# Six gate tiles of the second branch, made later as three pairs by seven quadrant products; piece sums moved to VectorE

## The chip, the cores and the metric

One core of a Trainium2 chip. The metric is device time in microseconds of one execution, as the median of repeated runs. The engines are TensorE (PE; its weight loads are PEld), VectorE (DVE), ScalarE (ACT), GpSimd (POOL) and SyncE (SP), whose queue issues almost all DMAs. All arithmetic is on float32 data; a matmul operand is split into a rounded high part and a low remainder (`wh`/`wl`, `xh`/`xl`, `th`/`tl` ...), and a product is three matmuls: high by high, high by low, low by high.

## The reference

One encoder layer over two sequences of 512 tokens with 1024 channels, with two memories of 256 tokens:

```python
xn = _rmsnorm(x, norm_mix);  h = xn @ w_in
u, q, k, v, xq, g = split(h)             # g: three gates of 1024 columns
y_s5 = s5(u)                             # state-space scan in two directions, gelu, glu
y_diff = diff_attention(q, k, v)         # 4 heads of two softmax maps, their difference
y_x = cross_attention(xq, memory)        # 4 heads
merged = sum(sigmoid(g[n]) * (branch[n] @ w_up[n]) for n in range(3))
x = x + merged @ w_out
gate, up = split(rmsnorm(x, norm_ffn) @ w_ffn_in)
x = x + (silu(gate) * up) @ w_ffn_out;   out = rmsnorm(x, norm_final)
```

## The kernel before, in words

Channels lie on the 128 partitions and tokens along the free axis: `xh[k]`, `xl[k]` (k from 0 to 7) are the normalised x, both sequences side by side in 1024 columns. An output tile of a projection (128 channels, both sequences) takes a weight tile of 512 KB (`weight`: DMA to `wf`, cast to `wh` on ScalarE, remainder `wl` on VectorE; two slots each) and 2 sequences by 8 k by 3 matmuls of 128x512.

The gates are 24 such tiles, drawn in order from the iterator `todo` (line 394); tile t is stored in HBM as `gD[t]`, and branch n uses tiles 8n to 8n+7. They serve as TensorE work beside what other engines do:

- `gates(n)` (400) makes n tiles at once. `NG = (7, 6, 3)` (42): 7 and 2 tiles ahead of the state-space scan, 4 between pieces of the scan, which VectorE does; then lines 420 to 424 put 0, 1 and 1 ahead of three steps of the scan's generator `s5` that make the scan's outputs (`behind()` lets a step's instructions follow the matmuls traced last). After them the outputs go to HBM (`yD`), are loaded again (`zu`, `zy`, lines 502 and 503), and pass through gelu into `zh`, `zl` (504 to 511); `gates(NG[2])`, three tiles, stands behind these lines and ahead of the projection by `w_glu`, which reads `zh`, `zl` by four contraction steps.
- Cross attention (690 to 726) runs 32 steps of scores, softmax, transpose and product, and between them `fill(n)` (590) takes n matmuls from `queue`, a list of generators. There the queue holds `xq` projections 1 to 3, two gate tiles, v for half the heads and the first q, 384 matmuls; a step takes 3 + 3 and what is left follows the last step.
- Differential attention has a second queue: q, k and v projections, three gate tiles and `merges()`. Ahead of its first scores (829) stand the first k projection and one gate tile. From line 679 to 921 TensorE keeps the written order (`PE.on`); elsewhere a planner with a cost model orders each engine's instructions.

`merges()` (794) holds the merge units of branches 0 and 2 (8 output tiles each, 24 matmuls a tile): load the gate (`gl`, from `gD`), multiply it with the product on VectorE (line 779), add into `mg[m]` on POOL (783). Those of branch 1 follow the queue, with 6 PSUM banks in place of 2. The operand of branch 1 is loaded and split in `merges()` (m = 2 to 5) and behind it. All loads of this kind, x parts and gate tiles share four slots of the tag `ld`.

Then come `w_out`, and the feed-forward input as 22 sweep steps. There a pair of tiles (one of gate, one of up, or two halves of channels by two sequences) is made by seven quadrant products in place of eight: operands 0 to 6 are four sums and differences of the quadrants of x beside three of them, weights A11, A12, A22 and S1 to S4 come from two weight tiles (`weights4`, 1003; the four sums of 128x512 on POOL, lines 1023 to 1026), and `running` (1120) accumulates four of the seven in one bank with copies between. A product is 4 k by 3 matmuls; a sweep step is 84.

Beside the sweep, `prepare` (457) makes the weights of 28 (m, p) pieces of the feed-forward output: load a piece (`raw`, four blocks of 128x128), four sums on POOL (`raw_sums`, 449, lines 452 to 455), split into `hl`, store to HBM (`wD`). The first 16 pieces store all seven weights, the next 12 the four sums alone. `half_piece` (489) does half a piece of the first kind or one of the second; it is called three times in a sweep step.

```python
    for n in (0, 1, 1):
        gates(n)
        with behind():
            next(s5)
```

Of the kernel before, what the change touches and what calls it, by code (L numbers as in the profile page):

```python
# [10 lines left out]
F32 = mybir.dt.float32  # L11
# [8 lines left out]
P = 128  # L20
# [20 lines left out]

NG = (7, 6, 3)

# [29 lines left out]
def encoder(ctx: ExitStack, tc: tile.TileContext, a, out):  # L73
# [319 lines left out]

    todo = iter(range(24))

# [52 lines left out]

    def raw_sums(raw):

        a21, a11, a12, a22 = (raw[:, i] for i in range(4))
        PO.tensor_tensor(out=a22, in0=a21, in1=a22, op=ALU.add)
        PO.tensor_tensor(out=a21, in0=a11, in1=a21, op=ALU.subtract)
        PO.tensor_tensor(out=a11, in0=a22, in1=a11, op=ALU.subtract)
        return PO.tensor_tensor(out=a12, in0=a12, in1=a11, op=ALU.subtract)

    def prepare(es_, todo_):
# [144 lines left out]
    def finish(g):  # L602
        while any(g is g_ for g_ in queue):
            fill(1)
# [78 lines left out]
    for i in range(-AHEAD, len(steps) + 1):  # L683
        if i + AHEAD < len(steps):
# [11 lines left out]
            es[i + AHEAD] = e  # L696
        fill(9 if i == 0 else 3)
        if 0 <= i < len(steps):
# [71 lines left out]
    def merge_units(n, b, m, first=False, last=False):  # L770
# [13 lines left out]
        if last:  # L784
            mgh[m] = slot("ms", [P, NT], F32R, f"mgh{m}")
            mgl[m] = slot("ms", [P, NT], F32R, f"mgl{m}")
            split(mgh[m], mgl[m], mg[m])
# [3 lines left out]
    b2_in = []  # L791
    b1_in = []

    def merges():
        res_.close()
        xp_es.close()
        open_tags(mes, side="right", mg=8, y=8)
        for m in range(KD):
            yield from merge_units(0, b0, m, first=True)
            if 3 <= m < 7:  # L800
                with tc.issue_after(last_s[0].ins):
                    merge_split(b2, 2, m - 3, "y", b2_in[m - 3])
            if 2 <= m < 6:
                b2_in.append(merge_load(2, m - 2))
        for m in range(KD):
            yield from merge_units(2, b2, m)
            if m == 2:
                open_tags(zes, side="right", z=4)
            if m in (2, 3):
                merge_split(b1, 1, m - 2, "z", merge_load(1, m - 2))  # L810
            elif m in (4, 5):
                b1_in.append(merge_load(1, m - 2))

# [10 lines left out]
    v1_ = v_units(1, v1)  # L824
    queue += [qk_units(1, True), dk[1], gate_units(), qk_units(2, True), dk[2], v1_, qk_units(3, True), dk[3], gate_units(),
              gate_units(), merges()]
    s0, ss, osb = {}, {}, {}

# [88 lines left out]
    aes.close()  # L917
    while queue:
        fill(24)
    assert next(todo, None) is None  # L920
    PE.on = False
    phase.close()
    ves.close()


    open_banks(mm=6, tr=2)
    open_tags(phase, ms=16)
    ves = ExitStack()
    open_tags(ves, y1=4)
    for t, yt in zip((2, 3), b1_in):  # L930
        merge_split(b1, 1, t, "y1", yt)
    for m in range(KD):
# [5 lines left out]


    zes.close()  # L940
    mes.close()
    ves.close()
    tes = ExitStack()
# [55 lines left out]

    H = 4 * P  # L1000
    last_ws = None

    def weights4(i):

        nonlocal last_w, last_ws
        a1, a2 = (wp.tile([P, DM], F32, tag="wf", name="wf") for _ in range(2))
        nc.sync.dma_start(a1, a["w_fg"][i])
        last_w = nc.sync.dma_start(a2, a["w_fu"][i])
        res = {}

        def sp(pool, src, sfx, *names):
            n = len(names) * H
            nonlocal last_s
            wh, wl = (pool.tile([P, DM], F32R, tag=t_ + sfx, name=t_, bufs=2) for t_ in ("wh", "wl"))
            last_s = split(wh[:, :n], wl[:, :n], src)
            for j, nm in enumerate(names):
                res[nm] = (wh[:, j * H : (j + 1) * H], wl[:, j * H : (j + 1) * H])

        sp(wp, a1, "", "A11", "A12")
        sp(wp, a2[:, H:], "", "A22")  # L1020
        yield res
        s12, s34 = (slot("ld", name="ws") for _ in range(2))
        PO.tensor_tensor(out=s12[:, :H], in0=a2[:, :H], in1=a2[:, H:], op=ALU.add)
        PO.tensor_tensor(out=s12[:, H:], in0=s12[:, :H], in1=a1[:, :H], op=ALU.subtract)  # L1024
        last_ws = PO.tensor_tensor(out=s34[:, H:], in0=a1[:, H:], in1=s12[:, H:], op=ALU.subtract)
        PO.tensor_tensor(out=s34[:, :H], in0=a1[:, :H], in1=a2[:, :H], op=ALU.subtract)
        yield
        sp(aps, s12, "s", "S1", "S2")
        sp(aps, s34, "s", "S3", "S4")
        yield  # L1030

# [30 lines left out]
    def product(ps, w, o, ks=range(4), on=False):  # L1062
        wh, wl = w
        for k in ks:
            th, tl = ops[k]
            ws_ = slice(k * P, (k + 1) * P)
            PE.matmul(ps, wh[:, ws_], th[:, o], start=(k == 0 and not on), stop=False, skip_group_check=on)
            PE.matmul(ps, wh[:, ws_], tl[:, o], start=False, stop=False, skip_group_check=on)
            PE.matmul(ps, wl[:, ws_], th[:, o], start=False, stop=(k == 3), skip_group_check=on)

    SEVEN = (("A11", 0), ("S2", 4), ("A12", 1), ("S3", 5), ("S1", 3), ("A22", 6), ("S4", 2))

    def products(i, w):
# [24 lines left out]
    last_sum = last_c = None  # L1098

# [791 lines left out]
```

## Time and profile before

| what | value |
|---|---|
| median of 3 runs | 1606.28 us (1604.17 to 1607.21) |
| profiled execution | 1605.93 us, its span 1604.1 us |
| mean granted TensorE clock | 0.998 |
| busy PE / PEld / DVE / ACT / POOL | 1578.0 / 1308.9 / 1116.0 / 648.0 / 495.2 us |
| HBM read, written | 165.16 MB, 71.27 MB |

The profile is of one execution. Busy time is the union of an engine's records; a matmul's record is longer than the spacing of matmuls, since they are pipelined, so that PE can read as busy without a gap at less than its best rate. In rows of groups stand the line, the engine, the operation, out<-in with shapes, the count, then busy us and mean ns of one, then the idle time of that engine before them and what ended it. In rows of waits stand who waited <- for whom, us in total, times, the longest. In rows in order of time stand start and duration in us.

### The profile page before, as it was taken

What the parts mean: (1) busy time and instruction counts of PE and PEld (TensorE: products, weight loads), DVE (VectorE), ACT (ScalarE), POOL (GpSimd) and SP (SyncE); (2) the same over time, 40 slices, a digit from 0 to 9 for tenths busy, and PEclk for the clock granted to TensorE, in tenths of its full rate; (3) what the DMA queues carried; (4) which work ended last, traced back from release to release, by engine and by line L of the source; (5) the groups of instructions that cost most, each with busy time, mean ns of one, the idle gap of its engine ahead of it and who ended that gap; (6) DMA issues with size and microseconds to landing.
All of it is one profiled execution on the core that took longest, in us unless ns stands there. A gap on an engine that the chain in (4) does not pass through costs nothing. (4 is left out here: it accounts for less than half of the span.)

```text
span 1604.1 us, 21458 instructions
## 1 busy us (share of the span) xinstructions
PE 1578.0 (98%) x7738; PEld 1308.9 (82%) x7738; DVE 1116.0 (70%) x1821; ACT 648.0 (40%) x1153; POOL 495.2 (31%) x415
## 2 busy tenths in 40 slices
PE   9999999999999999999999999999998999999998
PEld 7888888888898788778888888777776887888877
DVE  7978994086553876865555587777767666988864
ACT  6544213275442455754124354333333333233323
POOL 0010000000002320300452445555767334434673
PEclk9999999999999999999999999999999999999999
DMA  9554533573111211145534434445455323785412
GB/s 356 184 174 131 189 107 128 174 276 107 60 66 57 88 57 44 34 158 178 197 125 142 134 112 149 174 167 176 158 181 171 127 97 122 290 324 189 165 60 106
DMA packets 108842, 237.84 MB, mean 148 GB/s; under 512 B 14016, under 2 KB 45760, under 8 KB 108736
## 3 DMA queue, kind: packets, MB, share of 16 engines
q1 hardware_dynamic: 108160, 236.06, 43.4%
q8 instruction: 61, 1.00, 0.3%
q10 hardware_dynamic: 576, 0.41, 0.1%
q14 instruction: 45, 0.37, 0.1%
HBM read 165.16 MB, written 71.27 MB: 147 GB/s over the span
## 5 line engine op out<-in xcount | busy, mean ns | idle before, releaser
L66 PE MATMUL bkmm<-xh,wh 128*128 128x512 f32 x640 | 254.6, 398 | 0.0
L66 PE MATMUL bkmm<-xh,wl 128*128 128x512 f32 x640 | 250.4, 391 | 0.0
L66 PE MATMUL bkmm<-xl,wh 128*128 128x512 f32 x640 | 250.1, 391 | 0.0
L66 PE MATMUL bkmm<-th,wl 128*128 128x512 f32 (+1 forms) x621 | 237.3, 390 | 12.4 <-DVE wl L135 12.4
L66 PE MATMUL bkmm<-th,wh 128*128 128x512 f32 (+1 forms) x621 | 239.7, 390 | 1.8 <-ACT u L1128 1.0
L66 PE MATMUL bkmm<-tl,wh 128*128 128x512 f32 (+1 forms) x621 | 241.2, 388 | 0.0
L135 DVE TENSOR_TENSOR wl<-wf,wh 128x1024 fp32r<-128x1024 f32 (+2 forms) x134 | 153.0, 1141 | 77.5 <-ACT wh L134 73.0
L134 ACT CAST wh<-wf 128x1024 fp32r<-128x1024 f32 (+2 forms) x134 | 117.3, 875 | 171.1 <-PE bkmm L66 159.1
L744 POOL TENSOR_TENSOR t<-t,rs 128x512 f32<-128x512 f32 x16 | 26.6, 1665 | 461.1 <-DVE t L743 461.1
L66 PEld LDWEIGHTS bkmm<-th,wl 128*128 128x128 f32 x621 | 116.5, 188 | 40.7 <-DVE wl L135 17.0
L66 PE MATMUL bkmm<-th,w 128*128 128x512 f32 x432 | 141.0, 392 | 1.9 <-DVE nsq L1103 1.2
L66 PEld LDWEIGHTS bkmm<-xh,wh 128*128 128x128 f32 x640 | 120.3, 188 | 26.8 <-issue 3.5
L66 PEld LDWEIGHTS bkmm<-xh,wl 128*128 128x128 f32 x640 | 120.2, 188 | 26.0 <-issue 0.4
L66 PEld LDWEIGHTS bkmm<-xl,wh 128*128 128x128 f32 x640 | 120.4, 188 | 22.8
L66 PEld LDWEIGHTS bkmm<-th,wh 128*128 128x128 f32 x621 | 116.6, 188 | 27.2 <-ACT u L1128 2.1
L66 PEld LDWEIGHTS bkmm<-tl,wh 128*128 128x128 f32 x621 | 116.6, 188 | 24.0
L135 DVE TENSOR_TENSOR wl<-ws,wh 128x1024 fp32r<-128x1024 f32 x44 | 59.5, 1352 | 73.6 <-ACT wh L134 73.6
L66 PEld LDWEIGHTS bkmm<-th,w 128*128 128x128 f32 x432 | 80.9, 188 | 22.7 <-DVE nsq L1103 2.1
L134 ACT CAST wh<-ws 128x1024 fp32r<-128x1024 f32 x44 | 46.0, 1045 | 111.7 <-POOL ws L1024 105.4
L783 POOL TENSOR_TENSOR mg<-mg,gl 128x1024 f32<-128x1024 f32 x16 | 43.8, 2740 | 136.8 <-DVE gl L779 132.1
L66 PE MATMUL bkmm<-tl,w 128*128 128x512 f32 x216 | 84.1, 389 | 0.0
L66 PE MATMUL bkmm<-yh,wh 128*128 128x512 f32 x192 | 76.2, 397 | 0.0
(666 smaller groups left out, 3448.5 us busy)
## 6 DMA issues: line engine op xcount, KB each, us to landing
wf<-in_w_in SPq DMA_DIRECT2D x40, 512.0 KB, 3.7
wD<-hl SPq DMA_DIRECT2D x28, 512.0 KB, 3.2
w<-wD SPq DMA_DIRECT2D x28, 512.0 KB, 4.8
gD<-gt SPq DMA_DIRECT2D x24, 512.0 KB, 2.8
gl<-gD SPq DMA_DIRECT2D x24, 512.0 KB, 3.5
wf<-in_w_fg SPq DMA_DIRECT2D x22, 512.0 KB, 3.4
wf<-in_w_fu SPq DMA_DIRECT2D x22, 512.0 KB, 3.7
aD<-ac SPq DMA_DIRECT2D x44, 256.0 KB, 2.2
```

The costliest lines, as they stand in the source:

```text
L66: return self.put(self.eng.matmul(*args, **kw))
L134: h = S.copy(hi, src)
L135: l_ = V.tensor_tensor(out=lo, in0=src, in1=hi.bitcast(F32), op=ALU.subtract)
L744: PO.tensor_tensor(out=t2, in0=t2, in1=rope[1], op=ALU.mult)
L783: PO.tensor_tensor(out=mg[m], in0=mg[m], in1=gt, op=ALU.add)
```

## The change

Gate tiles 10 to 15 (branch 1, m = 2 to 7) leave `todo`. In their places: `NG` becomes (7, 6, 1), the loop ahead of the scan outputs (0, 0, 1), the queue of cross attention loses two gates and `fill` takes 4 + 4 a step, the gate ahead of the first differential scores goes. The normalised x of both sequences is stored in HBM (`xnD`, 4 MB) once it is made. When the merge units of branch 0 are done, the rest of the queue (branch 2) (`merges2`; `first_` is `merges0`, branch 0) runs alternately with `operands_x`, which loads x back and makes the seven operand pieces `xop` on VectorE and ScalarE. Behind the queue three pairs of tiles are made by `gate_pair`: 84 matmuls each, weights by `quad_weights` (the former `weights4`) with the four sums on VectorE, and `tanh` on ScalarE. The operand of branch 1 is then loaded and split, and its merge units follow. The output weights' piece sums in `prepare` run on VectorE in place of POOL; the feed-forward sweep itself keeps POOL for its weight sums.

```diff
-NG = (7, 6, 3)
+NG = (7, 6, 1)
+LATE = (2, 3, 4, 5, 6, 7)
...
+    xnD = drp.tile([NS, KD, P, L], F32, name="xnD")
...
         x_norm(0, norm[0], range(5, 8))
         _, bc = factor(ss1, DM)
+    nc.sync.dma_start(xnD[0].rearrange("k p n -> p k n"), xt[2])
...
         x_norm(1, bc, range(5, 8))
+    for i in range(4):
+        nc.sync.dma_start(xnD[1, 2 * i : 2 * i + 2].rearrange("k p n -> p k n"), xt[3][i])
...
-    todo = iter(range(24))
+    todo = iter([t for t in range(24) if t - KD not in LATE])
...
-    for n in (0, 1, 1):
+    for n in (0, 0, 1):
...
-    def raw_sums(raw):
+    def raw_sums(raw, eng=PO):
         a21, a11, a12, a22 = (raw[:, i] for i in range(4))
-        PO.tensor_tensor(out=a22, in0=a21, in1=a22, op=ALU.add)
+        eng.tensor_tensor(out=a22, in0=a21, in1=a22, op=ALU.add)
...
             if k == 7 or n_ == 0:
-                raw_sums(raws[n_])
+                raw_sums(raws[n_], V)
                 yield
             part(n_, 0, raws[n_])
             if n_ + 1 < len(todo_) and todo_[n_ + 1][2] == 4:
-                raw_sums(raws[n_ + 1])
+                raw_sums(raws[n_ + 1], V)
...
-    queue += [xq[1], gate_units(), xq[2], xq[3], v_units(0, v0), gate_units(), units(a["w_in"][4], xh, xl, dq0.__setitem__)]
+    queue += [xq[1], xq[2], xq[3], v_units(0, v0), units(a["w_in"][4], xh, xl, dq0.__setitem__)]
...
-        fill(9 if i == 0 else 3)
+        fill(9 if i == 0 else 4)
...
-        fill(3 if i < len(steps) else 15)
+        fill(4 if i < len(steps) else 15)
...
-    for _ in gate_units():
-        pass
...
+    finish(first_)
+    phase.close()
+    ves.close()
+    open_tags(phase, ta=8)
+    open_tags(qes, tb=4)
+    open_tags(ges, tt=1)
...
+    def operands_x():
+        rooms = [pieces_of("tb", 0, 2), pieces_of("ta", 3, 2), pieces_of("ta", 5, 2)]
+        for k in range(4):
+            x1_, x2_ = slot("ld", [P, 2, L], name="xa"), slot("ld", [P, 2, L], name="xb")
+            for s, t_ in enumerate((x1_, x2_)):
+                nc.sync.dma_start(t_, xnD[s, k::4].rearrange("a p n -> p a n"))
+            split(*next(rooms[0]), x1_)
+            t_ = slot("tt", [P, 4, L], name="tt")
+            V.tensor_tensor(out=t_[:, 0], in0=x2_[:, 0], in1=x1_[:, 0], op=ALU.subtract)
+            V.tensor_tensor(out=t_[:, 1], in0=x2_[:, 1], in1=t_[:, 0], op=ALU.subtract)
+            yield
+            V.tensor_tensor(out=t_[:, 2], in0=x2_[:, 1], in1=x2_[:, 0], op=ALU.subtract)
+            V.tensor_tensor(out=t_[:, 3], in0=x1_[:, 1], in1=t_[:, 1], op=ALU.subtract)
+            split(*next(rooms[1]), t_[:, 0:2])
+            split(*next(rooms[2]), t_[:, 2:4])
+            yield
+    parts = operands_x()
     while queue:
+        next(parts, None)
         fill(24)
+    for _ in parts:
+        pass
...
+    def gate_pair(m):
+        w = None
+        for r_ in quad_weights(a["w_in"][20 + KD + m], a["w_in"][20 + KD + m + 1], sps, V):
+            w = w or r_
+        g1, g2 = slot("ld", name="gp"), slot("ld", name="gp")
...
+        run = bank()
+        prod(run, "A11", 0)
+        u1 = kept_sum("u1")
+        p_ = bank()
+        prod(p_, "A12", 1)
+        gated(g1[:, :L], p_, u1)
+        prod(run, "S2", 4, True)
+        u2 = kept_sum("u2")
+        p5 = bank()
+        prod(p5, "S1", 3)
+        u4 = gps.tile([P, L], F32, tag="u1", name="u4")
+        V.tensor_tensor(out=u4, in0=p5, in1=u2, op=ALU.add)
+        prod(run, "S3", 5, True)
+        u3 = kept_sum("u3")
+        gated(g2[:, L:], p5, u3)
+        p_ = bank()
+        prod(p_, "S4", 2)
+        gated(g1[:, L:], p_, u4)
+        prod(run, "A22", 6, True)
+        S.activation(out=g2[:, :L], in_=run, func=AF.Tanh, scale=0.5)
+        for j, g_ in enumerate((g1, g2)):
+            nc.sync.dma_start(gD[KD + m + j], g_)
+
+    for m in LATE[::2]:
+        gate_pair(m)
+    for t in range(4):
+        hl = slot("tb", [P, 2, NT], F32R, f"1{t}")
+        b1[0][t], b1[1][t] = hl[:, 0], hl[:, 1]
+        split(*(b_[t] for b_ in b1), merge_load(1, t))
     for m in range(KD):
         for _ in merge_units(1, b1, m, last=True):
             pass
```

More of the change, by code (lines that the diff above doesn't have):

```diff
@@ L784, in merge_units @@
         if last:
[L785 to L786 removed]
+            hl = slot("ta", [P, 2, NT], F32R, f"mg{m}")
+            mgh[m], mgl[m] = hl[:, 0], hl[:, 1]
             split(mgh[m], mgl[m], mg[m])
@@ new lines, in encoder @@
+    gps = ges.enter_context(tc.tile_pool(name="gps", bufs=1, reuse_waits="tile"))
+    open_banks(mm=6, tr=2)
+    late = [slot("tc", [P, 4, L], F32R, n_) for n_ in ("lh", "ll")]
+    for k in range(0, 4, 2):
+        x_ = slot("ld", [P, 2, L], name="xc")
+        nc.sync.dma_start(x_, xnD[1, k + 4 : k + 6].rearrange("a p n -> p a n"))
+        split(*(t_[:, k : k + 2] for t_ in late), x_)
+        for j in range(2):
+            xop[2, k + j] = tuple(t_[:, k + j] for t_ in late)
+    H = 4 * P
@@ new lines, in quad_product, with prod, kept_sum, gated @@
+    def quad_product(op, ps, w, o, ks=range(4), on=False):
+        wh, wl = w
+        for k in ks:
+            th, tl = op(k, o)
+            ws_ = slice(k * P, (k + 1) * P)
+            PE.matmul(ps, wh[:, ws_], th, start=(k == 0 and not on), stop=False, skip_group_check=on)
+            PE.matmul(ps, wh[:, ws_], tl, start=False, stop=False, skip_group_check=on)
+            PE.matmul(ps, wl[:, ws_], th, start=False, stop=(k == 3), skip_group_check=on)
+    def gate_pair(m):
[3 more added lines that the diff above has]
+        g1, g2 = slot("ld", name="gp"), slot("ld", name="gp")
+        def prod(ps, nm, o, on=False):
+            quad_product(lambda k, o_: xop[o_, k], ps, w[nm], o, on=on)
+        def kept_sum(tag):
+            t_ = gps.tile([P, L], F32, tag=tag, name=tag)
+            S.copy(t_, run)
+            return t_
+        def gated(dst, p_, other):
+            V.tensor_tensor(out=dst, in0=p_, in1=other, op=ALU.add)
+            S.activation(out=dst, in_=dst, func=AF.Tanh, scale=0.5)
+        run = bank()
[20 more added lines that the diff above has]
+            nc.sync.dma_start(gD[KD + m + j], g_)
@@ L998, in operands @@
         return quad_split(i, xa_, xb_, quad_sums(xa_, xb_, third=third))
-    H = 4 * P
-    last_ws = None
     def weights4(i):
[L1005 to L1030, printed above, removed]
+        return quad_weights(a["w_fg"][i], a["w_fu"][i], aps, PO)
     ops = []
@@ L1062, in product @@
     def product(ps, w, o, ks=range(4), on=False):
[L1063 to L1069, printed above, removed]
+        quad_product(lambda k, o_: tuple(t_[:, o_] for t_ in ops[k]), ps, w, o, ks, on)
     SEVEN = (("A11", 0), ("S2", 4), ("A12", 1), ("S3", 5), ("S1", 3), ("A22", 6), ("S4", 2))
```

72 lines of the change are left out of this document (50 added, 22 removed).

## The prediction

> **What bounds the kernel now.** I read the page first, then the busy time by stretches, then the order of instructions where the edit lands.
>
> ```profile
> span 1604.1 us, 21458 instructions
> PE 1578.0 (98%) x7738; PEld 1308.9 (82%) x7738; DVE 1116.0 (70%) x1821; ACT 648.0 (40%) x1153; POOL 495.2 (31%) x415
> ...
> 312.50:345.20 32.70, 32.70 (x146) 27.08 (x146) 21.91 (x36) 16.71 (x23) 0.00 (x0) 1.00 0.74 262
> ...
> 757.00:801.00 44.00, 44.00 (x196) 36.13 (x196) 22.80 (x31) 9.86 (x19) 19.06 (x7) 1.00 0.59 192
> 991.00:1149.00 158.00, 153.62 (x673) 125.61 (x672) 118.38 (x144) 61.41 (x96) 93.72 (x93) 1.00 0.50 170
> 1149.00:1237.00 88.00, 79.17 (x340) 62.91 (x339) 63.11 (x72) 32.63 (x49) 68.26 (x72) 1.00 0.51 171
> 1256.00:1332.00 76.00, 76.00 (x337) 62.94 (x336) 49.32 (x65) 27.38 (x39) 28.24 (x20) 1.00 0.29 97
> ...
> 1560.00:1604.00 44.00, 36.92 (x272) 34.93 (x270) 19.43 (x42) 14.40 (x34) 17.42 (x21) 0.94 0.26 96
> ```
>
> The columns are the stretch, its length, then busy time with instruction count of PE, PEld, DVE, ACT, POOL, the granted clock, DMA share, GB/s. TensorE sets the end nearly everywhere. Its price of one 128x512 matmul is not the busy time of a record but the spacing: 76.00 us for 337 in 1256:1332, so 0.2255 us. At that price the two stretches before it should hold 700.6 and 390.2 matmuls and hold 673 and 340: 27.6 and 50.2 missing, 6.2 and 11.3 us, together 17.5 us of TensorE standing still. Those are the sweep steps of the feed-forward input in which the output weights are prepared as well.
>
> **The count of products.** Before, each of the six tiles is 2 sequences by 8 steps by 3 matmuls, 48; six are 288. After, each of three pairs is 7 products by 4 steps by 3, 84; three are 252. Minus 36 matmuls is 36 x 0.2255 = -8.1 us, if the late pairs run at TensorE's rate. In 1256:1332 the same pattern of seven products ran without a TensorE gap.
>
> **The tail of the scan branch.** One of the six gates leaves the loop around the scan outputs, two leave the line of three behind the last output (NG[2] from 3 to 1).
>
> ```profile
> 312.32 0.39 PE L1786 MATMUL bktr<-x,c_n 128*128 128x128 f32 x2
> ...
> 345.20 0.39 PE L66 MATMUL bkmm<-zh,wh 128*128 128x512 f32 x1
> ...
> L66 PE MATMUL bkmm<-xh,wh 128*128 128x512 f32 x48 | 18.8, 391 | 0.0
> ...
> L66 PE MATMUL bkmm<-zh,wh 128*128 128x512 f32 x32 | 12.1, 389 | 0.0
> ...
> 317.74 0.43 SPq L503 DMA_DIRECT2D zy<-yD  x1
> ...
> 322.08 1.28 DVE L504 SCALAR_TENSOR_TENSOR zy<-zu,vec,zy 128x1024 f32<-128x1024 f32 x1 [12.62 <-DMA zy<-yD]
> 327.43 1.22 DVE L135 TENSOR_TENSOR wl<-wf,wh 128x1024 fp32r<-128x1024 f32 x1
> 329.17 0.29 DVE L670 TENSOR_TENSOR lv<-lv 128x128 f32<-128x128 f32 x1
> 331.84 1.29 DVE L138 SCALAR_TENSOR_TENSOR zl<-zy,zh 128x512 fp32r<-128x512 f32 x2
> ...
> 348.24 0.68 DVE L138 SCALAR_TENSOR_TENSOR zl<-zy,zh 128x512 fp32r<-128x512 f32 x1
> ```
>
> The last scan matmul is at 312.32. Its output goes to HBM, comes back (zy, issued 317.74), and VectorE works through four tiles of gelu from 322.08 to 348.92 with hardly a pause: 36.6 us from 312.32. In between TensorE runs 3 x 48 = 144 gate matmuls, 32.5 us, and the gated projection starts at 345.20. So the cover is just as long as the chain; the three gates are no slack. Afterwards 48 matmuls, 10.8 us, lie over it. What can fill the rest is the projection itself on the tiles that are ready (331.84 is the first): two output tiles hold the four PSUM banks, so what must follow the last tile at 36.6 is 12 matmuls of its contraction step plus the 48 of the other two output tiles, 13.5 us. End of the projection 50.1 us behind the last scan matmul, against 10.8 + 96 x 0.2255 = 32.4 unhindered: 17.7 us lost, less up to 1.2 of gate weight split (327.43) that leaves VectorE's chain. Ends: 22.1 if nothing of the projection is pulled in (32.9 - 10.8), 13 if VectorE also sheds the small operations between. I take +17. The next projection cannot step in: its weights need a wh/wl slot, and both are held by the first two output tiles. The gate taken out of the loop is costed at nothing: it covered the loads of the third scan output, which then follows the second at once and may wait under 1 us for them, and the chain moves up with it.
>
> The Trainium skill (TensorE: Matmul & The Clock Gate, What's actually happening) says that after an idle window of about 3.4 us the clock is halved until about 3.4 us of activity: by it an estimated 1.7 us would come on top of this pause, a sum of 1614, inside the forecast's own range. The trace bears it out only at the kernel's ragged end, where the granted clock of the last 44 us reads 0.94.
>
> **Cross attention and the step to differential attention.** Two gates leave the filler queue, one the line ahead of the first scores. The filler per step rises to 8 of 288, which lasts for all the steps, so inside I cost it at nothing: the steps' own chains have more cover than before. What was behind is gone: TensorE now runs from the 48 matmuls of the first keys straight into the scores, in written order.
>
> ```profile
> 508.66 0.69 DVE L135 TENSOR_TENSOR rl<-t,rh 128x512 fp32r<-128x512 f32 x1 [3.49 <-ACT rh L134]
> ...
> 515.11 0.69 DVE L135 TENSOR_TENSOR rl<-t,rh 128x512 fp32r<-128x512 f32 x1 [3.20 <-ACT rh L134]
> ...
> 518.72 0.49 PE L66 MATMUL bktr<-rh 64*128 64x512 f32 x1
> ```
>
> The rotated keys are there at 509.35 (first sequence) and 515.80 (second). Without the gate the scores could start 10.8 us earlier, at 507.9: a stall of 1.4 us if the first half suffices, 7.9 if not. They read the first half only, so +1.5.
>
> **Operands and the second merge.** Operand pieces are made beside 44 us of merge units (757:801).
>
> ```profile
> L783 POOL TENSOR_TENSOR mg<-mg,gl 128x1024 f32<-128x1024 f32 x7 | 19.1, 2723 | 110.4 <-DVE gl L779 110.4
> ...
> L779 DVE SCALAR_TENSOR_TENSOR gl<-gl,bkmm 128x512 f32<-128x512 f32 x16 | 10.9, 684 | 14.8 <-PE bkmm L66 11.7 <-issue 3.1
> ...
> L135 DVE TENSOR_TENSOR yl<-yt,yh 128x1024 fp32r<-128x1024 f32 x4 | 5.4, 1347 | 5.8 <-ACT yh L134 5.8
> ...
> L973 DVE TENSOR_TENSOR ts<-x,ts 128x512 f32<-128x512 f32 x4 | 2.8, 689 | 0.1
> ...
> gl<-gD SPq DMA_DIRECT2D x24, 512.0 KB, 3.5
> ```
>
> Per k: three low parts of 128x1024 at 1.22 (327.43) and four differences at 0.689 (L973), 6.4 us; four times, 25.7 us on VectorE. It is busy 22.8 of 44 there, of which the four yl splits (5.4) move behind the pairs: 43.1 of 44 us then, so full, with the first pair's weights on top (A parts 1.9, sums 2.8 now on VectorE, S parts 2.4). The loads of a k hold two of the four ld slots that gl needs too; a load takes about 3.5 us (gl), two rounds of load and use some 11 us per k. Between nothing (all hidden) and 15 (the weights' 7.1 and as much again of collisions with POOL's 19.1) I take +4, since the early products need the early pieces only.
>
> **The pairs.** VectorE per pair: 7.1 for weights, three PSUM reads at 0.684, about 9.2 of 18.9 us. The wait that could grow is the S parts: sums, ScalarE's cast and the low part in a row, due 24 matmuls (5.4 us) after the pair begins; from the second pair on they are made a pair ahead, with two slots each. Gate stores and loads of the last pair lie ahead of its merge units. Branch-1 splits wait for slots that the last pair's second product frees, 13.5 us before its end. +1 (0 to 4). The sums of six tiles' worth of weights are new on VectorE, none on POOL. The normalised x goes out in five stores (4 MB) on SP in the first 100 us, and the next weight load queues behind each; 10 loads of 512 KB come back in the merge stage and at the first pair. +0.5 (0 to 3).
>
> **Piece sums on VectorE.** Four 128x128 operations for each of 28 pieces leave POOL.
>
> ```profile
> PE bkmm L66 <- DVE wl L135: 11.5, 9, 2.5
> ...
> POOL raw L452 <- DMA raw<-in_w_fo: 10.9, 2, 6.3
> ...
> L453 POOL TENSOR_TENSOR raw<-raw 128x128 f32<-128x128 f32 x13 | 11.9, 918 | 0.5
> L454 POOL TENSOR_TENSOR raw<-raw 128x128 f32<-128x128 f32 x12 | 9.0, 753 | 0.9
> ...
> L452 POOL TENSOR_TENSOR raw<-raw 128x128 f32<-128x128 f32 x13 | 8.3, 638 | 15.8 <-DMA raw<-in_w_fo 10.9 <-DVE hl L138 4.9
> ...
> L455 POOL TENSOR_TENSOR raw<-raw 128x128 f32<-128x128 f32 x12 | 7.9, 655 | 0.9
> ...
> 1208.54 2.28 DVE L135 TENSOR_TENSOR wl<-wf,wh 128x1024 fp32r<-128x1024 f32 x1
> ...
> 1208.33 1.41 POOL L1023 TENSOR_TENSOR ws<-wf 128x512 f32<-128x512 f32 x1 [0.26 <-DMA wf<-in_w_fu]
> ```
>
> TensorE's waits here are all on a late low weight part; the one at 1208.54 took 2.28 us instead of 1.22 while POOL summed weights. A piece takes POOL 2.96 us and would take VectorE 4 x 0.29 = 1.16. In 991:1149 that adds about 12 x 1.16 = 14 us to VectorE's 118 of 158: room. In 1149:1237 it adds 13 x 1.16 = 15 to 63: 78, where TensorE needs 4 x 84 x 0.2255 = 75.8 for its four sweep steps. So there VectorE itself comes to the edge, and the wait for a piece's load (10.9 us on POOL) would now hold VectorE, behind which PSUM reads and weight splits queue. I take back most of the first loss and under half of the second, 5 + 5 = -10; ends 0 and -17.5.
>
> The Trainium skill (SBUF — State Buffer, SBUF: two separate sides) has VectorE operations with two SBUF inputs and POOL exclude each other for whole instructions. The trace agrees (2.28 against 1.22). By it alone, the 31 us that POOL keeps in 1149:1237 (68.3 less 37.1 of piece sums) still stand against VectorE's 78, which would leave nothing of the second gain, a sum of 1617: this is rival (4) below, at its first step.
>
> **Sum.** -8.1 + 17 + 1.5 + 4 + 1 + 0.5 - 10 = +5.9. The profiled execution took 1605.93 (span 1604.1), beside a median of 1606.28: 1612.
>
> **Rivals.** (1) Faster: the tail stays covered, since the planner orders TensorE freely there. Against it: the held weight slots. It would need the pause to shrink to about 3 us: 1612 - 14 = 1598; it decides below about 8 us. (2) No change: POOL was the whole loss of the feed-forward stage, -17.5: 1604.5. For it: the gapless 1256:1332 with POOL at 28 of 76. (3) The operand pieces make VectorE or the ld slots the bound of the merge stage, +15: 1623. (4) VectorE, full or held by a piece's load, gives back the whole feed-forward gain: 1622.
>
> **How the numbers follow.** Forecast 0.42, with 1606 to 1618 of its own; (1) 0.20, (2) 0.13, (3) 0.12, (4) 0.13. About 0.2%, 3.2 us, is what a measurement of this kernel can tell from no change. Faster: (1) and the lower part of (2), 0.25. Same: the rest of (2) and the forecast's lower edge, 0.14. Slower: 0.61. The range reaches from below (1) to above (3): 1597 to 1627.
>
> **What would show it.** A TensorE pause of 13 to 22 us between the last scan matmul and the gated projection, ending on VectorE's zl; none means (1). From 12 to 22 sweep steps at 19.0 us each means (2). Waits of the first pair's S products on low parts longer than 5 us mean (3). VectorE idle for a raw load, or over 95% busy in the four-part pieces, means (4). The prediction is wrong if the pause is there but the rest gains over 25 us.

## The result and the profile after

The changed kernel takes 1643.88 us (median of four runs, 1640.57 to 1645.18) beside 1606.02 for the kernel before on the same chip: ratio 1.0234, 95% interval 1.0221 to 1.0247. It is slower by 37.9 us, where +6 was forecast and 1627 was the upper end of the range. The profiled execution took 1643.37.

The first lines of its page:

```profile
span 1641.6 us, 21503 instructions
PE 1584.7 (97%) x7702; PEld 1305.6 (80%) x7702; DVE 1197.1 (73%) x1993; ACT 673.4 (41%) x1184; POOL 421.8 (26%) x303
```

TensorE has 36 instructions fewer, as it should, and yet more busy microseconds (1584.7 against 1578.0): a part of its matmuls ran slower. VectorE has taken 81 us more, GpSimd 73 less.

To see where the time went, the span is cut at the same places of the program in both kernels: the last scan matmul, the end of the gated projection, the first differential scores, the last transposes of differential attention, the first matmul of w_out and of the feed-forward input. The busy time by stretches, kernel before, columns as in the prediction:

```profile
312.43:345.20 32.77, 32.77 (x147) 27.15 (x146) 21.91 (x36) 16.71 (x23) 0.00 (x0) 1.00 0.74 261
345.20:367.43 22.23, 22.23 (x102) 18.41 (x100) 13.74 (x28) 15.66 (x27) 0.00 (x0) 1.00 0.82 268
...
367.43:518.72 151.29, 151.26 (x834) 130.56 (x832) 78.27 (x206) 61.18 (x144) 11.96 (x8) 1.00 0.20 67
518.72:762.19 243.47, 243.41 (x1321) 198.01 (x1321) 173.43 (x321) 130.63 (x306) 37.91 (x24) 1.00 0.27 93
762.19:844.13 81.94, 81.94 (x363) 67.58 (x362) 44.54 (x55) 19.51 (x26) 40.59 (x15) 1.00 0.49 157
...
931.17:1351.00 419.83, 406.62 (x1790) 332.51 (x1789) 306.38 (x372) 161.06 (x241) 235.74 (x220) 1.00 0.43 148
```

The same view of the changed kernel:

```profile
301.84:320.10 18.26, 11.18 (x52) 8.95 (x50) 7.38 (x8) 7.09 (x11) 0.00 (x0) 0.88 0.91 321
320.10:342.51 22.41, 13.86 (x40) 10.13 (x40) 19.21 (x42) 15.29 (x22) 0.00 (x0) 0.72 0.50 201
342.51:358.31 15.80, 15.64 (x60) 12.37 (x61) 7.59 (x11) 6.86 (x12) 0.00 (x0) 0.89 0.42 134
723.40:771.08 47.68, 39.99 (x172) 31.02 (x170) 46.24 (x45) 15.79 (x20) 21.19 (x7) 1.00 0.62 204
771.08:834.91 63.83, 59.82 (x252) 47.94 (x253) 33.44 (x41) 25.10 (x36) 2.78 (x1) 0.97 0.32 109
...
358.31:478.97 120.66, 118.80 (x689) 103.57 (x687) 72.58 (x200) 55.38 (x136) 7.71 (x6) 1.00 0.20 66
478.97:723.42 244.45, 243.66 (x1320) 197.99 (x1321) 177.52 (x331) 130.37 (x306) 40.48 (x26) 1.00 0.26 88
723.42:880.50 157.08, 144.12 (x615) 114.85 (x614) 112.29 (x117) 55.56 (x72) 42.84 (x15) 0.99 0.47 157
...
967.54:1388.80 421.26, 408.38 (x1790) 331.73 (x1789) 324.77 (x483) 161.28 (x243) 160.97 (x108) 1.00 0.43 147
```

Each stretch is then compared with what the moved matmuls alone would make of it, at 0.2255 us each:

| Stretch | before | after | by the count | lost |
|---|---|---|---|---|
| up to the last scan matmul | 312.43 | 301.84 | -10.8 (one gate less) | 0.2 |
| scan tail and gated projection | 55.00 | 56.47 | -21.6 (two gates less) | 23.1 |
| cross attention, to the first scores | 151.29 | 120.66 | -32.5 (three gates less) | 1.8 |
| differential attention | 243.47 | 244.45 | 0 | 1.0 |
| rest of merges, pairs | 81.94 | 157.08 | +56.8 (252 matmuls) | 18.3 |
| w_out (from 844.13 and 880.50) | 87.04 | 87.04 | 0 | 0 |
| 21 sweep steps of the feed-forward input | 419.83 | 421.26 | 0 | 1.4 |
| what is left | | | 0 | -0.3 |

The last cut lies behind about 21 of the 22 sweep steps, some 20 us ahead of the stage's last matmul in both kernels. The lost parts make 45.5 us, less the 8.1 that the saved matmuls bring: 37.4, against 37.5 between the spans (1641.6 and 1604.1). Nine tenths of the loss lies in two stretches. The rows show their kinds: in the tail the granted clock reads 0.72 and TensorE is busy 13.86 of 22.41 us; in the second merge the clock is full and VectorE is busy 46.24 of 47.68.

In the tail the chain of waits, changed kernel (what waited, for whom, us in all, times, longest):

```profile
PE bkmm L68 <- ACT zh L139: 13.9, 3, 7.1
PE bktr L71 <- DVE rs L201: 1.7, 1, 1.7
```

the timeline of TensorE behind the last of those waits:

```profile
342.51 1.74 PE L68 MATMUL bkmm<-zh,wh 128*128 128x512 f32 x4 [1.90 <-ACT zh L139]
...
344.48 0.63 PE L68 MATMUL bkmm<-zh,wl 128*128 128x512 f32 x1
344.91 0.63 PE L68 MATMUL bkmm<-zl,wh 128*128 128x512 f32 x1
```

and the busy time of the two parts of that stretch:

```profile
342.51:346.70 4.19, 4.19 (x11) 3.25 (x12) 1.97 (x3) 1.80 (x4) 0.00 (x0) 0.59 0.00 0
346.70:358.31 11.61, 11.45 (x50) 9.12 (x50) 5.62 (x8) 5.06 (x10) 0.00 (x0) 1.00 0.57 182
```

The four waits make 15.6 us. Behind a pause two matmuls are 0.43 us apart (344.48 to 344.91) and the granted clock reads 0.59; from 346.70 on it is 1.00. Behind the last wait 60 matmuls took 15.80 us where 13.53 were due, 2.3 us more. Of these, 1.7 fall on the first 11, at the lowered clock; the other 0.6 came at full clock, 0.2 of it a wait for a weight cast. In the earlier lowered spells TensorE waited again right after, so that their cost would lie in a shorter wait; that is argued from this trace, no run separates it.

### The profile page after: what moved, and what is told of

Read it like the earlier page. It is cut to its first block, busy times and chain, and to the rows that moved or that the text cites. A ratio compares the mean times of both kernels' runs of the same rounds, so it can differ in the third digit from the quotient of the medians.

```text
span 1641.6 us, 21503 instructions
## 1 busy us (share of the span) xinstructions
PE 1584.7 (97%) x7702; PEld 1305.6 (80%) x7702; DVE 1197.1 (73%) x1993; ACT 673.4 (41%) x1184; POOL 421.8 (26%) x303
## 5 line engine op out<-in xcount | busy, mean ns | idle before, releaser
L68 PE MATMUL bkmm<-th,wh 128*128 128x512 f32 (+1 forms) x621 | 240.7, 391 | 10.6 <-ACT u L1227 10.6
L68 PE MATMUL bkmm<-xh,wh 128*128 128x512 f32 x544 | 217.7, 400 | 0.0
L68 PE MATMUL bkmm<-xh,wl 128*128 128x512 f32 x544 | 213.3, 392 | 0.0
L68 PE MATMUL bkmm<-xl,wh 128*128 128x512 f32 x544 | 212.7, 391 | 0.0
L68 PEld LDWEIGHTS bkmm<-xh,wh 128*128 128x128 f32 x544 | 102.2, 188 | 22.9 <-issue 3.5
L68 PEld LDWEIGHTS bkmm<-xh,wl 128*128 128x128 f32 x544 | 102.2, 188 | 22.4 <-issue 0.4
L137 DVE TENSOR_TENSOR wl<-ws,wh 128x1024 fp32r<-128x1024 f32 x50 | 64.5, 1290 | 76.0 <-ACT wh L136 76.0
L68 PEld LDWEIGHTS bkmm<-xl,wh 128*128 128x128 f32 x544 | 102.4, 188 | 18.9
L136 ACT CAST wh<-ws 128x1024 fp32r<-128x1024 f32 x50 | 52.0, 1044 | 101.5 <-POOL ws L1002 87.9
L68 PE MATMUL bkmm<-mg,wh 128*128 128x512 f32 x256 | 78.4, 389 | 0.0
```

What stands on the lines that cost most here:

```text
L68: return self.put(self.eng.matmul(*args, **kw))
L136: h = S.copy(hi, src)
L137: l_ = V.tensor_tensor(out=lo, in0=src, in1=hi.bitcast(F32), op=ALU.subtract)
```

## The experiments

Each label starting with b_ is an edit of the kernel before, each with a_ an edit of the changed kernel. Times are medians, ratios are to the kernel before on the same chip. The kernel before read 1605.31 to 1606.97 in the sets of runs, so a difference of 2 us between medians of two chips is not clear of the noise. In the code, `...` stands for lines left out.

**b_tail: the uncovered tail by itself.**

```
-NG = (7, 6, 3)
+NG = (7, 6, 1)
...
-    for n in (0, 1, 1):
+    for n in (0, 0, 1):
...
-  ... qk_units(3, True), dk[3], gate_units(),
+  ... qk_units(3, True), dk[3], *(gate_units() for _ in range(4)),
```

> The kernel before with only the tail of the scan branch changed: one gate out of the loop around the scan outputs and two out of the line of three behind the last output, all three put in the filler of differential attention; number of matmuls unchanged, no late pairs, piece sums on GpSimd. Theory (the uncovered scan tail costs 23 us by itself: about 16 of waits and 7 of a lowered TensorE clock): 1606 + 23 = 1629. Rival (the pause alone, as predicted, 17): 1623. Rival (the tail loses time only because the late pairs' stores and the planner's other choices crowd it): 1606 to 1612.

Measured 1631.04, 1.0156 (1.014 to 1.0171): 25.7 us slower than 1605.31. The interval, 22.5 to 27.5, holds the theory's 23 and leaves out 17. Its stretches:

```profile
301.45:320.29 18.84, 11.17 (x51) 8.94 (x49) 7.46 (x8) 7.19 (x11) 0.00 (x0) 0.89 0.91 302
320.29:359.15 38.86, 29.50 (x101) 22.62 (x101) 26.81 (x52) 21.91 (x32) 0.00 (x0) 0.79 0.49 179
```

The same pause and lowered clock, without late pairs and without sums on VectorE. So the tail's loss needs nothing but the three gates gone from there.

**a_2pairs: the cover put back.**

```
-NG = (7, 6, 1)
-LATE = (2, 3, 4, 5, 6, 7)
+NG = (7, 6, 3)
+LATE = (4, 5, 6, 7)
```

> The changed kernel with two late pairs instead of three; the two freed gate tiles go back behind the last scan output (line of three again). 84 matmuls of a pair are replaced by 96 of two gates, +2.7 us. Theory (the two gates behind the last output are what covers the tail): the 23.4 us lost there go, 1643.9 - 23.4 + 2.7 and a further 1 to 2 less for the pair's own stalls, about 1622. Rival (the loss of the tail is in the order of work, not in its cover): 1643.9 + 2.7 = 1646.

Measured 1623.50, 1.011 (1.0096 to 1.0124), 20.4 below the changed kernel. The tail:

```profile
302.21:334.98 32.77, 32.77 (x148) 27.14 (x147) 21.44 (x35) 16.05 (x21) 0.00 (x0) 1.00 0.76 260
334.98:357.20 22.22, 22.22 (x101) 18.40 (x100) 14.29 (x28) 16.31 (x29) 0.00 (x0) 1.00 0.83 269
```

Busy throughout at full clock, as before, and near the 1622 that was expected. The rival, a loss in the order of work, is out.

**a_memlate, a_memzt: why the last tile came late.** The prediction put the last tile 36.6 us behind the last scan matmul; TensorE waited for it until 342.51, which is 40.7. The transfers of the third and fourth scan input took longer: the DMA issues in the matching stretches, the kernel before and then the changed one (KB each, median us to landing):

```profile
zu<-uD SPq DMA_DIRECT2D x2, 512.0 KB, 3.2
```

```profile
zu<-uD SPq DMA_DIRECT2D x2, 512.0 KB, 6.2
```

The first edit holds the memory's norm behind the last low part; the second puts its loads into the slots of the scan inputs:

```
...
-    with behind():
+    with tc.issue_after(last_z[1].ins):
```

> The changed kernel with the norm of the memory (its square root on ScalarE with two table loads of 1.28 us, two products of 1.23 us on VectorE) held until the last low part of the scan output is made, instead of only until the last gate. Theory (with two gates fewer this small work falls into the gelu chain and lengthens it by 3 to 5 us): 1639 to 1641. Rival (the chain is as long as its own work, or the memory operands become late for cross attention): 1644 or above.

```
-        rs_, bc = factor(sums(a["memN"], "ld"), DM)
+        rs_, bc = factor(sums(a["memN"], "zt"), DM)
```

> The changed kernel with the four loads of the memory's norm in the slots of the scan's inputs instead of the general load slots, so that they can start only when the last scan outputs are through. Theory (those loads make the third and fourth scan input land after 5.4 and 7.0 us instead of 3.3 and 3.2, and their squares and the square root stand in ScalarE's queue): the last tile 3 to 4 us sooner, 1639 to 1641. Rival (VectorE's and ScalarE's chain over the four tiles is as long by itself): 1643 to 1645, and above if cross attention now waits for the memory.

Measured 1643.58 (1.0238, 1.0221 to 1.0255) and 1645.90 (1.0244, 1.0227 to 1.0261): neither brought time. In the first the loads and the square root still ran in the middle of the chain; only the two products moved, and the last wait ended 0.7 us sooner, counted from the last scan matmul. The second is the clear one (timeline):

```profile
334.48 2.36 ACT L139 ACTIVATE zh<-zy 128x512 fp32r<-128x512 f32 x4
...
342.79 1.06 ACT L241 ACTIVATE tk<-tk 128x1024 f32<-128x1024 f32 x1 [1.56 <-DMA tk<-in_memN]
...
343.97 0.69 ACT L533 ACTIVATE sg<-bkmm,bh 128x512 f32<-128x512 f32 x1
...
346.93 0.79 PE L68 MATMUL bkmm<-zh,wh 128*128 128x512 f32 x1 [4.41 <-ACT wh L136]
```

All casts were through at 336.84, 35.0 us behind the last scan matmul and 6.1 us sooner than in the changed kernel (342.98, or 41.1): the memory's early loads and the work that follows them on the engines were what made the tile late. The loads alone are not the whole of it: with those loads out of the way the two transfers still took 5.1 us (median), against 3.2 in the kernel before. In exchange ScalarE now waits for the memory's loads in the middle of the projection (tk), drains its banks behind them (sg), casts the third weight late, and TensorE waits 4.4 us for it. What one wait gave back went to the next in line.

**a_clk: the clock.** 58 matmuls whose results nobody reads, placed behind the last gate and behind the second and third tile.

> The changed kernel with 58 matmuls of 512 columns, whose results nobody reads, offered to TensorE in the waits of the scan tail, so that its clock isn't lowered there. If only the matmuls behind the last wait count (before it a slower TensorE only waits less): 4 us faster, 1640. If the whole 7 us of lowered clock count: 1637. If the clock is lowered for another reason than the waits: no gain or slower, 1644 to 1650.

Measured 1649.29, 1.0264 (1.0249 to 1.028): slower. The number is that of the third forecast, but not for its reason. The planner put none of the 58 into the first wait, which stayed (6.5 us), and all of them into 331.73 to 350.17. There they covered the later waits, but stood ahead of projection matmuls that were ready: the third tile's casts began at 336.36, its matmuls at 343.82. The run shows only that the projection's end then ran at full clock:

```profile
350.17:364.67 14.50, 13.94 (x62) 11.18 (x61) 6.47 (x10) 6.39 (x11) 0.00 (x0) 1.00 0.50 155
```

What a held clock is worth was not separated from the pause; the 1.7 us is read from the changed kernel's trace alone.

**a_mgV and a_noops: VectorE in the second merge.** VectorE's groups there, changed kernel (count, then busy us, mean ns):

```profile
L137 DVE TENSOR_TENSOR ol<-tt,oh 128x1024 fp32r<-128x1024 f32 x8 | 11.5, 1436 | 0.0
L137 DVE TENSOR_TENSOR wl<-wf,wh 128x512 fp32r<-128x512 f32 x6 | 10.7, 1778 | 0.0
...
L947 DVE TENSOR_TENSOR tt<-xb,xa 128x512 f32<-128x512 f32 x3 | 4.9, 1641 | 1.4 <-DMA xb<-xnD 1.4
...
L137 DVE TENSOR_TENSOR wl<-wf,wh 128x1024 fp32r<-128x1024 f32 x1 | 3.4, 3424 | 0.0
```

A low part of 128x512 took 1778 ns, one of 128x1024 3424. The timeline shows when:

```profile
724.04 2.40 POOL L789 TENSOR_TENSOR mg<-mg,gl 128x1024 f32<-128x1024 f32 x1 [93.36 <-DVE gl L785]
...
724.53 2.98 DVE L137 TENSOR_TENSOR ol<-tt,oh 128x1024 fp32r<-128x1024 f32 x1
...
728.04 1.21 DVE L137 TENSOR_TENSOR ol<-tt,oh 128x1024 fp32r<-128x1024 f32 x1
```

The same operation takes 2.98 us while GpSimd adds and 1.21 when it doesn't. The first edit moves that add to VectorE, the second leaves out part of the operand work:

```
-            PO.tensor_tensor(out=mg[m], in0=mg[m], in1=gt, op=ALU.add)
+            V.tensor_tensor(out=mg[m], in0=mg[m], in1=gt, op=ALU.add)
```

> The changed kernel with the adds to the merged tile (128x1024, two SBUF inputs) on VectorE instead of GpSimd. Theory (in the second merge VectorE is full because each of GpSimd's 7 adds of about 3 us holds one of its operations for about 2 us, 13.5 in all, while the adds cost VectorE 7 x 1.22 = 8.5): 3 to 6 us faster, 1638 to 1641. Rival (VectorE is full by its own work, and 8.5 more make it the bound): 1648 to 1652.

```
-            V.tensor_tensor(out=t_[:, 0], in0=x2_[:, 0], in1=x1_[:, 0], op=ALU.subtract)
...
-            split(*next(rooms[2]), t_[:, 2:4])
+            split(*next(rooms[1]), x2_)
+            xop[5, k], xop[6, k] = xop[3, k], xop[4, k]
```

> The changed kernel with part of the operand work left out beside the second merge: the four differences per step and one of the two casts and low parts of the pieces 3 to 6 (pieces 5 and 6 are replaced by 3 and 4, and those by the second sequence); 15.8 us less on VectorE, the same matmuls. Theory (VectorE full is what costs the second merge its 9.8 us): 8 to 11 us faster, 1633 to 1636. Rival (the loads and the ld slots hold it): 1641 to 1644.

Measured 1638.28 (1.0200, 1.0185 to 1.0215) and 1637.13 (1.0193, 1.0179 to 1.0206): 5.6 and 6.8 faster than the changed kernel. The first is as expected; the second lies 1.1 us above its theory's range and below its rival's. a_mgV in the same groups:

```profile
L137 DVE TENSOR_TENSOR ol<-tt,oh 128x1024 fp32r<-128x1024 f32 x8 | 9.8, 1219 | 0.0
...
L789 DVE TENSOR_TENSOR mg<-mg,gl 128x1024 f32<-128x1024 f32 x7 | 8.5, 1218 | 0.0
L137 DVE TENSOR_TENSOR wl<-wf,wh 128x512 fp32r<-128x512 f32 x6 | 4.1, 685 | 0.0
```

Against these durations the four groups of the changed kernel had lost 8 x 0.217 + 6 x 1.093 + 3 x 0.957 + 2.2 = 13.4 us to being held; the adds cost VectorE 8.5 instead. The stretch of 168 merge matmuls (37.9 us by the count) comes down from 47.68 to 42.86 us, and without the operand work to 39.73:

```profile
722.53:762.26 39.73, 39.06 (x171) 31.40 (x170) 26.91 (x30) 10.76 (x14) 19.67 (x7) 1.00 0.70 236
```

So a full VectorE is the cause there: with less work on it and the same loads, the stretch lies 1.8 us above the count instead of 9.8, and those 1.8 are all that is left for the loads and ld slots, the rival. Taking GpSimd's hold away brings about half (4.8 us), after paying the 8.5 us of the adds.

**b_vsum, a_posum: the piece sums alone.** One argument in two calls, `raw_sums(raws[n_], V)` against `raw_sums(raws[n_])`.

> The kernel before with only the piece sums moved from GpSimd to VectorE. Forecast of the prediction: 10 us faster, 1596. Theory now (the sweep steps of the feed-forward input hang on a ring: VectorE's late low part of A22 holds the second weight buffer, its reload lands late, GpSimd's weight sums and the S parts follow late; the piece sums only change which engine's queue stands in it): no gain, 1603 to 1609, and TensorE's waits move from the low parts to ScalarE's kept copies.

> The changed kernel with the piece sums back on GpSimd. By the prediction's term 10 us slower, 1654. By the ring theory the same within 3 us, 1641 to 1647.

Measured 1607.38, 1.0011 (1.0002 to 1.002), and 1640.69, 1.0217 (1.0203 to 1.0231). The move brought no gain in either kernel. In the kernel before it cost about 2 us (interval 0.3 to 3.2); in the changed kernel the 3.2 us are not clear of the noise, the two intervals overlap. TensorE's waits in the feed-forward input, b_vsum:

```profile
PE bkmm L66 <- ACT u L1128: 9.4, 9, 1.9
PE bkmm L66 <- DVE wl L135: 2.1, 5, 0.8
```

Before it was 11.5 on wl, as the prediction shows; in the changed kernel it is 10.6 on u and 2.2 on wl, and in a_posum 11.0 on wl again. The wait changed its name and about kept its size. How that comes about can be followed in one step of the changed kernel, whose low part of A22 is the first row:

```profile
1076.66 0.69 DVE L137 TENSOR_TENSOR wl<-wf,wh 128x512 fp32r<-128x512 f32 x1
...
1077.38 0.33 SPq L986 DMA_DIRECT2D wf<-in_w_fu  x1
...
1081.13 3.12 POOL L1001 TENSOR_TENSOR ws<-wf 128x512 f32<-128x512 f32 x1 [6.26 <-DMA wf<-in_w_fu]
...
1086.78 1.05 ACT L136 CAST wh<-ws 128x1024 fp32r<-128x1024 f32 x1 [3.02 <-POOL ws L1002]
...
1090.57 0.63 ACT L1301 ACTIVATE ac<-gf 128x512 f32<-128x512 f32 x1 [2.73 <-DVE gf L1300]
...
1092.45 0.58 ACT L1227 COPY u<-bkmm 128x512 f32<-128x512 f32 x1
...
1093.08 0.50 PE L68 MATMUL bkmm<-th,wh 128*128 128x512 f32 x1 [1.37 <-ACT u L1227]
```

The up weights are loaded only when VectorE has made that low part; GpSimd, freed of the piece sums, stands idle for that load; its sums and ScalarE's cast follow in a row. VectorE's part of the gate (gf) comes behind that cast's low part, and ScalarE's own order puts gate, casts and the kept copy (u), for which TensorE waits, behind gf. GpSimd's first weight sum over the same 20 steps, in the kernel before and in b_vsum (idle time and what ended it at the end):

```profile
L1023 POOL TENSOR_TENSOR ws<-wf 128x512 f32<-128x512 f32 x20 | 31.9, 1597 | 61.9 <-DMA wf<-in_w_fu 61.9
```

```profile
L1023 POOL TENSOR_TENSOR ws<-wf 128x512 f32<-128x512 f32 x20 | 38.6, 1930 | 121.7 <-DMA wf<-in_w_fu 115.2 <-ACT u L1128 6.5
```

Piece sums of 80.6 us left GpSimd there, and its wait for that load grew by 53.3.

**b_a22, b_wq, b_wqv, b_pre, b_prev: what holds the load.** Low part of A22 on GpSimd:

```
-            last_s = split(wh[:, :n], wl[:, :n], src)
+            if names == ("A22",):
+                S.copy(wh[:, :n], src)
+                PO.tensor_tensor(out=wl[:, :n], in0=src, in1=wh[:, :n].bitcast(F32), op=ALU.subtract)
...
```

> The kernel before with the low part of A22 (128x512) on GpSimd instead of VectorE in the feed-forward input; piece sums stay on GpSimd. Ring theory (the second weight buffer comes free late because that low part stands in VectorE's queue): the sweep steps come down towards 19.04 us, 8 to 17 us faster, 1589 to 1598. Rival (GpSimd's own queue, with 1.3 us more in it each step, is the bound): 1606 to 1612.

A22 in a buffer of its own, with the piece sums on GpSimd and on VectorE:

```
-        sp(wp, a2[:, H:], "", "A22")
+        q_ = aps.tile([P, H], F32, tag="wq", name="wq", bufs=1)
+        nc.sync.dma_start(q_, a["w_fu"][i][:, H:])
+        sp(wp, q_, "", "A22")
```

> The kernel before with the A22 half of the up weights loaded a second time into a buffer of its own (256 KB more per sweep step), so that its late low part no longer holds the second weight buffer; piece sums on GpSimd. Moving that low part to GpSimd didn't test this, since it stood in GpSimd's queue just as late. Ring theory: 8 to 17 us faster, 1589 to 1598. Rival (the queues of GpSimd and VectorE set the sweep step, not the buffer): within 4 us of 1606.

> The same buffer for A22 with the piece sums on VectorE too. If the ring hid the gain of the piece sums, this is faster than the run with the buffer alone by several us (towards 1588, no stalls left). If VectorE's queue is the bound with the sums in it, it is slower than that run by 2 to 5 us.

The next weights asked for earlier, again with both places of the sums:

```
...
+        if 1 <= i < KFF - 3:
+            nxt_w = all7(i + 1)
...
```

> The kernel before, with the weights of the next sweep step of the feed-forward input asked for ahead of the gate arithmetic and the second piece of this step, so that the planner gives their casts, low parts and sums the earlier places in each engine's queue; piece sums on GpSimd. Theory (the place of A22's low part in VectorE's queue sets when the next up weights are loaded, and with that the late S parts): 8 to 15 us faster, 1591 to 1598. Rival (the sum of work on GpSimd and VectorE sets the step, not its order): 1603 to 1609, or slower, since PSUM banks are then read later.

> The same order with the piece sums on VectorE as well. If the order was what hid their gain: as fast as the run with the sums on GpSimd or faster, down to 1590. If VectorE is the bound with them: slower than that run by 3 to 8 us.

| Run | us | ratio, interval |
|---|---|---|
| b_a22 | 1617.13 | 1.0066 (1.0051 to 1.0081) |
| b_wq | 1610.49 | 1.0027 (1.0018 to 1.0036) |
| b_wqv | 1598.84 | 0.9956 (0.9942 to 0.9969) |
| b_pre | 1606.07 | 0.9998 (0.9988 to 1.0007) |
| b_prev | 1608.33 | 1.0012 (1.0002 to 1.0021) |

The ring theory as it was put is not borne out: b_a22 came out slower than both of its forecasts, b_wq at the upper edge of its rival's. b_a22 made the low part no sooner, behind GpSimd's other work, and GpSimd later. In b_wq the load of the up weights waited for the low part of A11 and A12 instead (that ends at 1007.97, the load is issued at 1008.00): one holder exchanged for another. b_pre and b_prev tested nothing, since the load kept its place: it is issued 11.4 and 6.9 us behind that of the gate weights by turns in the kernel before, 11.6 and 6.9 in b_pre, 11.9 and 7.7 in b_prev as in b_vsum. What stands is b_wqv: with the buffer, moving the sums to VectorE is worth 11.65 us (1610.49 to 1598.84, on one chip), and the version is 7.2 us faster than the kernel before (interval 5.0 to 9.3). In it TensorE's waits on low parts make 7.1 us instead of 11.5, and the kept copies are hardly waited for (0.6):

```profile
PE bkmm L66 <- DVE wl L135: 7.1, 8, 1.4
```

Why the two edits help only together stays open. GpSimd's wait for the load does not tell it: in b_wq, where the move then paid, that wait was even longer than the 61.9 us of the kernel before:

```profile
L1025 POOL TENSOR_TENSOR ws<-wf 128x512 f32<-128x512 f32 x20 | 27.6, 1379 | 120.1 <-DMA wf<-in_w_fu 120.1
```

**a_best: all causes taken away at once.** Two late pairs, the adds on VectorE, the buffer for A22.

> The changed kernel with two late pairs (tail covered), the adds to the merged tile on VectorE, and A22 in a buffer of its own in the feed-forward input (piece sums on VectorE). If the causes add up: 1623.5 - 5 - 7 = about 1611, still slower than before, because the operand work and the pairs' own waits cost more than the 24 matmuls that are left of the saving (5.4 us). Rival (they share VectorE's fill and more goes than the sum): 1600 or less.

Measured 1610.84, 1.0029 (1.002 to 1.0038); the sum as written makes 1611.5. So the causes add up within the noise, and two late pairs do not pay even then: 12 us above b_wqv, which has no late pair, and 4.8 above the kernel before.

## Why the prediction was wrong

The direction held; the size was off by 32 us, and three of its terms carry 30.5 of that. In the table "measured" is the loss of a stretch against the count of matmuls at 0.2255 us; the first row is that count and not a measurement.

| Term | predicted | measured |
|---|---|---|
| 36 matmuls fewer | -8.1 | -8.1 (count) |
| scan tail (with the gate out of the loop) | +17 | +23.3 |
| first differential scores (with that attention) | +1.5 | +2.8 |
| operands, pairs, stores | +5.5 | +18.3 |
| feed-forward input | -10 | +1.4 |
| rest | 0 | -0.3 |

**Tail: mechanism right, size short.** The pause came where it was foretold, and b_tail and a_2pairs show it alone and undone. What follows the last tile was right to the count, 60 matmuls. The mis-sized terms are the last tile, whose matmuls began 40.7 us behind the last scan matmul instead of 36.6, and the 60 matmuls, 2.3 us longer than their count, 1.7 of it for a lowered clock that the prediction named and left out of its sum. The chain was taken over from the trace before with its loads; when gates go, what stood behind them (the memory's loads and the work on them) moves up too and crowds it. One detail of the forecast failed: the pause ends on ScalarE's zh, not on zl.

The Trainium skill (TensorE: Matmul & The Clock Gate, What's actually happening) was cited for 1.7 us. On its size the trace agrees: the first 11 matmuls behind the last wait took 4.19 us where 2.5 were due. On its condition, an idle window of about 3.4 us, it does not, if that means a pause of such a length: that wait was 1.9 us, and the clock was lowered all the same (from 339.60 to 342.90 TensorE was busy for 1.40 of 3.30 us at a clock of 1.00, from 343.00 to 346.30 the clock reads 0.50).

**First scores:** two waits of 2.3 us together, both on the rotated keys, within the ends given.

**Operands: rival (3) was the case.** The step that failed is the one that took +4 between 0 and 15 "since the early products need the early pieces only". It priced the pieces by what TensorE needs of them and not by what stands behind them on VectorE: the PSUM reads of the merge (`gl`), without which no bank comes free. TensorE's waits on them make 5.6 us there in the changed kernel and 0.7 in a_noops. The same paragraph had VectorE at 43.1 of 44 us, at durations measured when it was alone, and kept the collisions with GpSimd for the upper end of its range. In the prediction's own rows GpSimd's add ran at 2723 ns and a low part at 1347 ns against 1.22; on a full VectorE that hold costs, 13.4 us of it. Of the 18.3 us, 9.8 fell in the second merge, 7.0 in the pairs (63.83 against 56.8), where +1 was taken, and 1.5 behind them. In the pairs TensorE was not busy for 4.0 us, and a spell of clock 0.50 (780.00 to 783.30) explains about 1.7 more; no run takes these apart. Rival (3)'s sign, waits of the first pair's S products on low parts of more than 5 us, did not show (one wait of 1.1): the sign named the wrong place.

The Trainium skill (SBUF — State Buffer, SBUF: two separate sides) has that mutual exclusion; the prediction used it for the feed-forward stage only, and the trace agrees here too, with 2.98 us beside GpSimd's add and 1.21 without it, and a_mgV is what taking the add away brings.

**Feed-forward input: rival (4) by its price, not by its mechanism.** VectorE was neither full (70.05 of 88 us in 1185.40 to 1273.40, where 78 was forecast) nor once held by a piece's load. The step that failed is "TensorE's waits here are all on a late low weight part", read as GpSimd's work, so that moving that work would bring 10 us. Moved alone it brought none (b_vsum): TensorE's wait went over to the kept copies. In the trace those parts come at the end of a chain through the reload of the up weights, in which GpSimd's sums are one link, and in the kernel before GpSimd already stood idle 61.9 us for that load. That this chain is the cause is argued from the order in the trace; the edits that were to break it did not gain alone, so the cause stays open. The 17.5 us that were to be won back are also high: they count missing matmuls, while the same two rows have TensorE not busy for 13.2 us, 11.5 of it on low parts.

**The range.** Rivals (3) and (4) were priced one at a time. Nothing in them excludes each other, and both came: by the prediction's own prices 5.9 + 11 + 10 = 26.9, 1633, beyond the end of its range.

## What to carry to other kernels

Before an engine is relieved, try the relief alone. GpSimd waited 61.9 us for a load and its relief brought nothing here; it waited 120.1 us for the same load in b_wq and its relief brought 11.65 us. So neither how busy an engine is nor what ends its idle time was enough to forecast the gain. Filler work is priced by the chain that it covers; take it from a place where the engine that replaces it has slack, and expect the work behind it to move up into that chain. On a full engine, count operations at the durations that they have beside their neighbours and not alone, and put what others wait for, the PSUM reads, ahead in the sum. Where two rivals do not exclude each other, the range has to hold both.

## What the runs showed of the hardware

Two matmuls at the lowered clock were 0.43 us apart, not quite twice 0.2255. In or just behind pauses of 7.1, 5.0 and 1.9 us the clock was lowered each time, the short one too. Less was enough in the first pair: waits of 1.00 and 1.11 us, one soon after the other, left TensorE busy for 1.42 of 3.30 us (776.60 to 779.90), and from 780.00 to 783.30 the granted clock reads 0.50. In both short cases the clock read 1.00 until the end of the waits and was then lowered for about 3.4 us. An add of 128x1024 took 3.0 us on GpSimd (21.19 for 7, beside a busy VectorE) and 1.22 on VectorE, and while GpSimd did it VectorE's operations with two SBUF inputs were held, at most for 2.2 us (3.42 instead of 1.22).
